# Where tiles lie in SBUF: matmul operands at the bottom, and one 8 KB room for three stages, in a one-core fp32 decoder trunk

## The chip, the cores and the metric

The kernel runs on one core of a Trainium2 chip. The metric is the device time of one execution in microseconds, of which three were taken: 1074.09, 1074.84 and 1077.22, so the median is 1074.84 us. A profile of one execution stands beside them. Its span, from the first to the last instruction, is 1070.4 us.

## The reference

Two layers work on 256 tokens of 1024 channels. Each layer is a half SwiGLU, a mixer and another half SwiGLU, all with a residual. The first mixer is a diagonal state-space model (S5), the second is sparse attention (NSA) over keys and values made after the first layer.

```python
def _swiglu(x, w_in, w_out):
    a, b = jnp.split(x @ w_in, 2, axis=-1)
    return (jax.nn.silu(a) * b) @ w_out
...
    for layer in range(DEPTH):                      # DEPTH = 2, d_model 1024, d_ff 2816
        h = h + 0.5 * _swiglu(_rmsnorm(h, ffn1_norm[layer]), ffn1_w_in[layer], ffn1_w_out[layer])
        u = _rmsnorm(h, mix_norm[layer])
        if layer < N_A_LAYERS:
            h = h + _s5_mixer(u, ...)
        else:
            h = h + _nsa_mixer(u, kv, w_qg[b], q_norm[b], w_o[b], rel_bias)
        h = h + 0.5 * _swiglu(_rmsnorm(h, ffn2_norm[layer]), ffn2_w_in[layer], ffn2_w_out[layer])
        if layer == N_A_LAYERS - 1:
            kv = _shared_kv(h, ...)
```

All of it is fp32.

## The kernel before

**The product of three.** fp32 accuracy comes from splitting each operand into a high and a low part and summing three products (`mm3`, L112 to L117): high activations by high weights (L115), high by low (L116), low by high (L117). The activations are the stationary operand, 128 channels by 128 tokens, loaded by a weight load (PEld) before each matmul. The weights are the moving operand, 512 columns for a full matmul.

**The weights.** Each 1 MB granule comes by one DMA (L70) into one of two buffers `raw`. ScalarE rounds it into `whi` (L86 without a gain, L96 with one) and VectorE subtracts the rest into `wlo` (L92, L99). `whi` and `wlo` have five buffers of 4 KB per partition each, and each buffer holds two slabs of 512 columns.

**The SwiGLU stage** (`ffn`, L177) runs four times: ffn1 of layer 0, ffn2 of layer 0, ffn1 of layer 1, ffn2 of layer 1. Each goes over 11 chunks of 256 hidden channels. A chunk makes 48 matmuls `mm<-whi,xT` and `mm<-wlo,xT` into two accumulators (L222 to L227), from `xT`, the transposed activations (16 KB per partition, high and low). After the fifth slab (k = 4) it also turns the gate product `g` of the chunk before: four transposes on PE (L190), a rounding copy on ScalarE (L140) and a subtraction on VectorE (L141) into `gT` (4 KB, two buffers in the pool `ffn`). At the end of the chunk come the 24 matmuls of the chunk before with `gT` as the stationary operand, `o<-whi,gT` and `o<-wlo,gT`, into four accumulators (`second`, L200). The order on each engine is the order of issue. In the first three passes `background` puts steps of other work into the gaps between slabs: the preparation of S5, the bias tables, what follows the shared projections.

**S5** (`s5`, L487) copies its turned input into `uT` (8 KB, pool `s5r`), drives the states from it (L529, `uT` moving), and closes with a gated product whose stationary operand `yh` lies in the same tile as `xT` (matmuls `ga`, four accumulators). **Attention** (`attention`, L798) turns the probabilities of one head group (L913), copies them into `pt0` (ScalarE, L918) and `pt1` (VectorE, L916), two buffers of 2 KB each, and multiplies them, as the moving operand, by the values (L922). Its output projection has the stationary operand `oT` (matmuls `mm<-..,oT` and `x<-..,oT`, four accumulators). The shared projections (L700, L701) use `xT` again; a third of them goes into the accumulators `kv`.

**Where tiles lie.** Pools are stacked in the order in which they are opened, tiles within a pool in the order of their first use, and a pool that is closed leaves its room to the next one. Counted in KB per partition from the lowest tile of the kernel, the sizes in the code give this layout:

| tile | before |
|---|---|
| `h` (residual), `ident`, `gains` | 0 to 8.7 |
| `xT`, and `yh` of S5 | 8.7 to 24.7 |
| `raw`, two buffers | 24.7 to 40.7 |
| `whi`, five buffers | 40.7 to 60.7 |
| `wlo`, five buffers | 60.7 to 80.7 |
| small tiles | 80.7 to 82.0 |
| `oT` of attention | 138.6 to 154.6 |
| `gT`, last pass | 126.5 to 134.5 |
| `gT`, second and third pass | 169.3 to 177.3 |
| `gT`, first pass | 198.5 to 206.5 |
| `uT` of S5 | 186.2 to 194.2 |
| `pt0`, `pt1` of attention | 198.4 to 206.4 |

Of the kernel before, what the change touches and what calls it, by code (L numbers as in the profile page):

```python
# [9 lines left out]
F32 = mybir.dt.float32  # L10
# [6 lines left out]
P = 128  # L17
# [15 lines left out]
def kernel(ctx: ExitStack, tc: tile.TileContext, A, out):  # L33
    nc = tc.nc
    V, S, G, T = nc.vector, nc.scalar, nc.gpsimd, nc.tensor

    pers = ctx.enter_context(tc.tile_pool(name="pers", bufs=1))
    rawp = ctx.enter_context(tc.tile_pool(name="rawp", bufs=2))
    hip = ctx.enter_context(tc.tile_pool(name="hip", bufs=5))
    lop = ctx.enter_context(tc.tile_pool(name="lop", bufs=5))  # L40
# [12 lines left out]
    # ---- constants and gains  # L53
# [10 lines left out]
    # ---- weights: each granule is split exactly into hi + lo parts as it arrives, scaled by the gain of its rows  # L64
# [13 lines left out]
    def split_half(raw, j, w, gain, k0, eng="av"):  # L78
        """eng: which engines round and subtract"""
# [39 lines left out]
    def gemm(acc, xT, gen, kts=KT, lead=False):  # L119
        """acc[t] = x[t] @ W over kts slabs; lead: token tile 0 goes first in groups of four slabs"""  # L120
# [8 lines left out]
    # ---- 1/rms of the rows of one token tile of h, from its two halves  # L129
# [14 lines left out]
    # ---- h^T as hi and lo parts, channels on partitions, with 1/rms of its rows  # L144
    class Acts:
        def __init__(self, hc):
            self.h = hc
            self.xT = pers.tile([P, 2, KT, 256], F32R, name="xT")
            self.rs = small.tile([P, 2], F32, name="rs", bufs=4)
            self.ss = small.tile([P, 4], F32, name="ss")  # L150
# [15 lines left out]
    def background(bg, n):  # L166
        """n steps of other work, queued behind what has been issued so far"""
# [8 lines left out]
    # ---- res += 1/2 SwiGLU(rmsnorm(h)); done(t, half) once a half of token tile t of res is complete  # L176
    def ffn(x, gi, w_in, w_out, res, perm=False, bg=None, steps=1, done=None, first=()):  # L177
        with tc.tile_pool(name="ffn", bufs=2) as fp, tc.tile_pool(name="ps_a", bufs=1, space=PSUM) as pa:
            xT, rs = x.xT, x.rs
            acc2 = [[pa.tile([P, 512], F32, name=f"o{t}{hf}") for hf in range(2)] for t in range(2)]  # L180
# [3 lines left out]
            def transposed(g):  # L184
                """g^T of one chunk, hi and lo, tokens in natural order"""
                gT = fp.tile([P, 2, 2, 256], F32R, name="gT")
# [31 lines left out]
            for c in range(NCH):  # L218
# [4 lines left out]
                else:  # L223
                    for k in range(KT):
# [3 lines left out]
                        if k == 4:  # L228
                            gT = transposed(prev)
# [12 lines left out]
            second(NCH - 1, transposed(prev))  # L242

    # ---- S5 in chunks of four tokens: discretisation, rotation tables, and stationary operands
# [6 lines left out]
    def s5_prepare(kp, sp, W):  # L251
# [36 lines left out]
        def exp_parts(x):  # L288
            """2^n and exp(r) - 1 with x = n ln2 + r."""
# [53 lines left out]
        def products(x, y, t4_):  # L343
            """x_re y_re, x_im y_im, x_re y_im, x_im y_re"""
# [120 lines left out]
    # ---- h += S5(rmsnorm(h)); token 4 c + 2 t + e is in row 64 e + c of token tile t  # L465
# [651 lines left out]
```

## Time and profile before

| | |
|---|---|
| runs | 1074.09, 1074.84, 1077.22 us |
| span of the profiled execution | 1070.4 us |
| median of the runs less this span | 4.4 us |
| VectorE busy | 708.6 us (66%) |
| ScalarE busy | 574.7 us (54%) |
| GpSimd busy | 180.5 us (17%) |
| HBM read | 165.54 MB, 160 GB/s over the span with what is written |

The profiled execution has no time of its own beside the span; what lies around the span is taken to be the 4.4 us by which the median of the runs exceeds it. The duration of a matmul in the profile is longer than its place in the stream: successive matmuls overlap, so their pace is read from the distance of their starts, and the durations serve to tell groups apart.

### The profile page before, as it was taken

What the parts mean: (1) busy time and instruction counts of PE and PEld (TensorE: products, weight loads), DVE (VectorE), ACT (ScalarE), POOL (GpSimd) and SP (SyncE); (2) the same over time, 40 slices, a digit from 0 to 9 for tenths busy, and PEclk for the clock granted to TensorE, in tenths of its full rate; (3) what the DMA queues carried; (4) which work ended last, traced back from release to release, by engine and by line L of the source; (5) the groups of instructions that cost most, each with busy time, mean ns of one, the idle gap of its engine ahead of it and who ended that gap; (6) DMA issues with size and microseconds to landing.
All of it is one profiled execution on the core that took longest, in us unless ns stands there. A gap on an engine that the chain in (4) does not pass through costs nothing.

```text
span 1070.4 us, 14818 instructions
## 1 busy us (share of the span) xinstructions
PE 1002.3 (94%) x5553; PEld 807.9 (75%) x5553; DVE 708.6 (66%) x1403; ACT 574.7 (54%) x1051; POOL 180.5 (17%) x185
## 2 busy tenths in 40 slices
PE   7978999988879899999999999999977899999998
PEld 6766877876657688887887888887866678888886
DVE  5999755949875465656757555655688866656553
ACT  6443566643335464655665555554786656545451
POOL 6375100305732000000005100000203220000000
PEclk9988999999989999999999999999988999999999
DMA  6553544420328865555464455554303146555551
GB/s 237 183 187 118 197 158 140 163 91 24 137 103 205 331 201 193 197 176 181 170 221 158 158 187 173 191 197 145 100 1 118 40 138 214 170 186 197 185 176 72
DMA packets 27912, 171.74 MB, mean 160 GB/s; under 512 B 4544, under 2 KB 4992, under 8 KB 9024
## 3 DMA queue, kind: packets, MB, share of 16 engines
q1 hardware_dynamic: 26192, 164.77, 44.5%
q0 software_dynamic: 1648, 6.03, 2.2%
q8 instruction: 43, 0.70, 0.3%
q14 instruction: 29, 0.24, 0.1%
HBM read 165.54 MB, written 5.24 MB: 160 GB/s over the span
## 4 chain that ended last, share of the span: by engine, by line
PE 73%; DVE 14%; DMA 4%; ACT 4%; POOL 3%; issue 2%; SPq 0%; ACTq 0%; POOLq 0%; DVEq 0%
PE mm L115 14%; PE mm L116 13%; PE mm L117 13%; PE o L117 7%; PE o L115 7%; PE o L116 7%; DMA raw<-in_w_in_dram 4%; DVE wlo L99 4%; DVE wlo L92 2%; PE tr L190 1%; DVE w L544 1%; ACT whi L96 1%; DVE Pt L906 1%; ACT Pt L895 1%; PE tr L913 1%
## 5 line engine op out<-in xcount | busy, mean ns | idle before, releaser
L99 DVE SCALAR_TENSOR_TENSOR wlo<-raw,gains,whi 128x512 fp32r<-128x512 f32 (+2 forms) x408 | 295.7, 759 | 130.6 <-ACT whi L96 126.7
L96 ACT ACTIVATE whi<-raw,gains 128x512 fp32r<-128x512 f32 (+2 forms) x408 | 267.3, 699 | 187.2 <-PE mm L117 60.8
L115 PE MATMUL mm<-whi,xT 128*128 128x512 f32 (+2 forms) x800 | 313.5, 392 | 4.5 <-ACT whi L96 3.5
L117 PE MATMUL mm<-whi,xT 128*128 128x512 f32 (+2 forms) x800 | 307.1, 384 | 0.0
L116 PE MATMUL mm<-wlo,xT 128*128 128x512 f32 (+2 forms) x800 | 306.8, 384 | 0.3 <-DVE wlo L99 0.3
L92 DVE TENSOR_TENSOR wlo<-raw,whi 128x512 fp32r<-128x512 f32 x192 | 135.0, 743 | 95.3 <-ACT whi L86 95.1
L86 ACT ACTIVATE whi<-raw 128x1024 fp32r<-128x1024 f32 x104 | 108.8, 1057 | 133.6 <-PE mm L117 62.1
L115 PEld LDWEIGHTS mm<-whi,xT 128*128 128x128 f32 x800 | 151.1, 189 | 36.0 <-ACT whi L96 4.8
L117 PEld LDWEIGHTS mm<-whi,xT 128*128 128x128 f32 x800 | 150.9, 189 | 29.8
L116 PEld LDWEIGHTS mm<-wlo,xT 128*128 128x128 f32 x800 | 151.2, 189 | 28.4 <-DVE wlo L99 1.1
L115 PE MATMUL o<-whi,gT 128*128 128x512 f32 x352 | 143.0, 406 | 9.5 <-ACT gT L140 9.5
L117 PE MATMUL o<-whi,gT 128*128 128x512 f32 x352 | 141.6, 404 | 8.1 <-DVE gT L141 7.9
L116 PE MATMUL o<-wlo,gT 128*128 128x512 f32 x352 | 141.4, 402 | 0.0
L115 PEld LDWEIGHTS o<-whi,gT 128*128 128x128 f32 x352 | 67.7, 192 | 27.5 <-ACT gT L140 11.9
L117 PEld LDWEIGHTS o<-whi,gT 128*128 128x128 f32 x352 | 67.6, 192 | 26.3 <-DVE gT L141 10.1
L116 PEld LDWEIGHTS o<-wlo,gT 128*128 128x128 f32 x352 | 67.7, 192 | 15.7
L235 ACT ACTIVATE g<-mm,rs 128x256 f32<-128x256 f32 x88 | 40.7, 471 | 27.7 <-PE mm L117 27.6
L236 DVE SCALAR_TENSOR_TENSOR g<-mm,rs,g 128x256 f32<-128x256 f32 x88 | 41.9, 483 | 19.9 <-ACT g L235 19.4
L141 DVE TENSOR_TENSOR gT<-tr,gT 128x512 fp32r<-128x512 f32 (+1 forms) x55 | 36.4, 661 | 25.9 <-ACT gT L140 25.6
L140 ACT ACTIVATE gT<-tr 128x512 fp32r<-128x512 f32 (+1 forms) x55 | 33.3, 605 | 33.4 <-PE tr L190 26.7
L137 POOL TENSOR_TENSOR rs<-ms,nhalf 128x1 f32<-128x1 f32 x12 | 7.2, 600 | 231.7 <-DVE ms L136 231.6
L895 ACT ACTIVATE Pt<-Pt,mx 128x128 f32<-128x128 f32 (+1 forms) x64 | 28.4, 445 | 6.4 <-DVE mx L890 6.3
(311 smaller groups left out, 1009.1 us busy)
## 6 DMA issues: line engine op xcount, KB each, us to landing
raw<-in_w_in_dram SPq DMA_DIRECT2D x87, 1024.0 KB, 4.9
raw<-in_w_out_dram SPq DMA_DIRECT2D x44, 1024.0 KB, 4.9
raw<-in_w_kv_dram SPq DMA_DIRECT2D x6, 1024.0 KB, 4.8
raw<-in_w_glu_dram SPq DMA_DIRECT2D x4, 1024.0 KB, 4.8
raw<-in_w_o_dram SPq DMA_DIRECT2D x4, 1024.0 KB, 4.9
revd<-rev POOLq DMA_DIRECT2D x8, 384.0 KB, 15.0
raw<-in_w_qg_dram SPq DMA_DIRECT2D x6, 512.0 KB, 3.6
B<-revd POOLq DMA_DIRECT2D x1, 2048.0 KB, 13.2
```

Source lines behind the costliest of these rows:

```text
L86: Last.act = S.activation(hi, r, AF.Copy)
L92: i = el.tensor_tensor(out=lo[:, c], in0=r[:, c], in1=hi[:, c].bitcast(F32), op=ALU.subtract)
L96: Last.act = S.activation(hi[:, c], r[:, c], AF.Identity, scale=g_)
L99: i = V.scalar_tensor_tensor(out=lo[:, c], in0=r[:, c], scalar=g_, in1=hi[:, c].bitcast(F32), op0=ALU.mult, op1=ALU.subtract)
L115: T.matmul(ps, lhsT=xh, rhs=wh, start=start, stop=False)
L116: T.matmul(ps, lhsT=xh, rhs=wl, start=False, stop=False)
L117: Last.pe = T.matmul(ps, lhsT=xl, rhs=wh, start=False, stop=stop_)
L140: i = S.activation(dst_hi, src, AF.Copy)
L141: V.tensor_tensor(out=dst_lo, in0=src, in1=dst_hi.bitcast(F32), op=ALU.subtract)
L235: Last.act = S.activation(sl, acc[t][:, 0:256], AF.Silu, scale=rs[:, t:t + 1])
L236: Last.dve = V.scalar_tensor_tensor(out=g[:, t, :], in0=acc[t][:, 256:512], scalar=rs[:, t:t + 1], in1=sl, op0=ALU.mult, op1=ALU.mult)
L895: S.activation(Pt[:, r, br], Pt[:, r, br], AF.Exp, scale=-1.0, bias=mx[:, c:c + 1], accum_out=sm[:, c:c + 1])
```

## The change

Nothing that is computed changes, and no instruction is added or taken out by intent. Three things are done to the tiles.

1. A new pool `low` is opened first. It takes `xT` (and `yh`) out of `pers`, and a new tile `turned` of 8 KB. After it come `whi` (`hip`) and `wlo` (`lop`), then `pers` with `h`, `ident` and `gains`, then `raw`.
2. `turned` is one room for three stages. Each pass of `ffn` takes it for `gT`, the chunk's parity choosing the half; S5 takes it for `uT`; attention takes it for its four turned blocks, used in rotation.
3. The pool `s5r` and the tiles `gT`, `pt0`, `pt1` of the old pools go.

```diff
+    low = ctx.enter_context(tc.tile_pool(name="low", bufs=1))
+    hip = ctx.enter_context(tc.tile_pool(name="hip", bufs=5))
+    lop = ctx.enter_context(tc.tile_pool(name="lop", bufs=5))
     pers = ctx.enter_context(tc.tile_pool(name="pers", bufs=1))
     rawp = ctx.enter_context(tc.tile_pool(name="rawp", bufs=2))
-    hip = ctx.enter_context(tc.tile_pool(name="hip", bufs=5))
-    lop = ctx.enter_context(tc.tile_pool(name="lop", bufs=5))
...
+    def turn_room():
+        return low.tile([P, 2, 1024], F32R, name="turned")
...
-            self.xT = pers.tile([P, 2, KT, 256], F32R, name="xT")
+            self.xT = low.tile([P, 2, KT, 256], F32R, name="xT")
...
+            gTs = turn_room()
...
-            def transposed(g):
-                gT = fp.tile([P, 2, 2, 256], F32R, name="gT")
+            def transposed(c, g):
+                gT = gTs[:, c % 2].rearrange("p (i f c) -> p i f c", i=2, f=2)
...
-                            gT = transposed(prev)
+                            gT = transposed(c - 1, prev)
...
-            second(NCH - 1, transposed(prev))
+            second(NCH - 1, transposed(NCH - 1, prev))
...
-        with tc.tile_pool(name="s5r", bufs=1) as rp, tc.tile_pool(name="s5w", bufs=2) as wp, \
+        with tc.tile_pool(name="s5w", bufs=2) as wp, \
...
-            uT = rp.tile([P, NG, NC], F32, name="uT")
+            uT = turn_room().bitcast(F32).rearrange("p b (g c) -> p (b g) c", c=NC)
...
-            yh = pers.tile([P, 2, KT, 256], F32R, name="xT")
+            yh = low.tile([P, 2, KT, 256], F32R, name="xT")
...
+            pt_room, turn = turn_room().bitcast(F32).rearrange("p b (k c) -> p (b k) c", c=512), [0]
...
-                        pts.append(tp.tile([P, 512], F32, name=f"pt{br}"))
+                        pts.append(pt_room[:, turn[0] % 4])
+                        turn[0] += 1
```

By the sizes in the code the layout becomes, in the same count: `xT` 0 to 16, `turned` 16 to 24, `whi` 24 to 44, `wlo` 44 to 64, `h` 64 to 72, `ident` and `gains` to 72.7, `raw` 72.7 to 88.7. Everything above is 8 KB higher than before, less what `gT`, `uT`, `pt0` and `pt1` took there. `oT`, `g`, and the operands of S5 other than `uT` stay high. The other lines of the diff take out comments.

## The prediction

> **What bounds the kernel now.** I read the page's head and slices first, then the chain of waits, then stretches of one pass, then single matmuls in order of time.
>
> ```profile
> span 1070.4 us, 14818 instructions
> PE 1002.3 (94%) x5553; PEld 807.9 (75%) x5553; DVE 708.6 (66%) x1403; ACT 574.7 (54%) x1051; POOL 180.5 (17%) x185
> PE   7978999988879899999999999999977899999998
> by line: PE mm L115 13.7%; PE mm L116 13.5%; PE mm L117 13.4%; PE o L117 7.0%; PE o L115 7.0%; PE o L116 6.9%; DMA raw<-in_w_in_dram 4.0%; DVE wlo L99 3.6%; issue 1.9%; DVE wlo L92 1.6%; PE tr L190 1.4%; DVE w L544 1.3%; ACT whi L96 1.1%; D
> ```
>
> TensorE is busy 94% of the span, and the six groups of SwiGLU matmuls make 61.5% of the chain that ended last. Outside the first four slices, S5 (slices 9 to 12) and attention (30 to 32) the row of TensorE stands at 8 or 9. Two stretches from inside the passes show what the other engines have left:
>
> ```profile
> 390.00:500.00 110.00, 110.00 (x495) 90.20 (x495) 66.88 (x104) 60.43 (x90) 0.00 (x0) 1.00 0.55 190
> 901.00:918.00 17.00, 17.00 (x78) 13.91 (x77) 9.91 (x16) 8.90 (x14) 0.00 (x0) 1.00 0.55 186
> ACT whi L86 <- PE mm L117: 62.1, 38, 6.8
> ACT whi L96 <- PE mm L117: 60.8, 49, 2.5
> ACT whi L86 <- PE o L117: 36.5, 25, 1.5
> ACT whi L96 <- PE o L117: 24.7, 17, 5.4
> ```
>
> In a chunk of 17 us TensorE has no gap, while VectorE works 9.91 us, ScalarE 8.90 and the DMA engines 55%. ScalarE waits 62.1 + 60.8 + 36.5 + 24.7 = 184.1 us for TensorE to give weight buffers back: the weights are ahead. So a pass costs what its matmuls cost, and the question is whether their price hangs on where their operands lie.
>
> **The one thing the change can reach.** All full matmuls have one shape, 128 by 128 stationary and 512 columns moving, yet they fall into two classes:
>
> ```profile
> L115 PE MATMUL kv<-whi,xT x16: 389/389/389, 527.5 to 537.7; 128*128 128x512 f32 x16
> L115 PE MATMUL mm<-whi,xT x800: 276/389/797, 7.9 to 1052.9; 128*128 128x512 f32 x147, 128*128 128x256 f32 x9, 128*128 128x304 f32 x4
> L115 PE MATMUL o<-whi,gT x352: 388/396/792, 34.5 to 1065.4; 128*128 128x512 f32 x176
> L115 PE MATMUL x<-whi,oT x16: 390/392/398, 851.5 to 876.6; 128*128 128x512 f32 x16
> 531.79 0.39 PE L116 MATMUL kv<-wlo,xT 128*128 128x512 f32 x1
> ...
> 538.14 0.39 PE L117 MATMUL kv<-whi,xT 128*128 128x512 f32 x1
> 622.07 0.39 PE L115 MATMUL o<-whi,gT 128*128 128x512 f32 x1
> ...
> 627.68 0.39 PE L115 MATMUL mm<-whi,xT 128*128 128x512 f32 x1
> ...
> 629.07 0.39 PE L115 MATMUL mm<-whi,xT 128*128 128x512 f32 x1
> 851.51 0.39 PE L115 MATMUL x<-whi,oT 128*128 128x512 f32 x1
> ...
> 854.31 0.39 PE L115 MATMUL x<-whi,oT 128*128 128x512 f32 x1
> 271.96 0.39 PE L117 MATMUL ga<-whi,xT 128*128 128x512 f32 x1
> ...
> 273.10 0.39 PE L116 MATMUL ga<-wlo,xT 128*128 128x512 f32 x1
> ```
>
> (min/median/max in ns; then starts in us.) With `xT` as the stationary operand the median is 389 ns, with `gT` 396, with `oT` 392. The pace shows the same. From 531.79 to 538.14 lie 28 steps of the `kv` run: 6.35 / 28 = 226.8 ns. From 622.07 to 627.68 lie the 24 of one `o` run: 5.61 / 24 = 233.8 ns. From 851.51 to 854.31 lie 12 of `oT`: 2.80 / 12 = 233.3 ns. After an `o` run the first six `xT` matmuls still take 1.39 us (627.68 to 629.07) instead of 6 x 226.8 = 1.36.
>
> What tells the classes apart? Not the moving weights: all read the same buffers `whi` and `wlo`. Not the number of accumulators: `ga` alternates over four, as `o` and `oT` do, and runs 271.96 to 273.10 in 5 steps at 228 ns, the fast class. Not the shape of the stationary tile: `oT` is laid out as `xT` is. Left is the place: `xT` lies at 8.7 to 24.7 KB, `gT` at 126 KB and above, `oT` at 138.6 KB. The trace cannot say whether height, or distance from the weights at 40.7 to 80.7 KB, makes the difference. The change ends both: `gT` comes to 16 to 24 KB, wholly inside the room that `xT` has today, just below the weights.
>
> [...]
>
> **The sum, part by part.**
>
> *`gT` low.* 24 x (233.8 - 226.8) = 0.168 us per run of 24. The recovery behind it gives up to 0.03 us more; I take 0.02, since a run still begins after a wait in places. Together 0.188 us a chunk. How many of the 44 runs count? The `o` lines hold 7.0 + 7.0 + 6.9 = 20.9% of the chain, 223.7 us; by 0.2338 that is 957 matmuls, 39.9 runs. Some of these ran at a lowered clock in the first pass (0.93 between 50 and 100 us, row below), which inflates the figure, so 38: 38 x 0.188 = 7.1 us. Nothing is late in its place: the next chunk's weights have the 184.1 us of waiting in hand, and per 17 us only 0.19 of it is used.
>
> *`xT`, `whi`, `wlo` low.* All move down by 8.7 to 16.7 KB. The 16 `kv` rows of L115 go over eight slabs, which is four of the five `whi` buffers, and all of them take 389, so the place of the moving weights has shown no price and I take 0. Bounds: the recoveries vanish altogether, as much again as the 0.02 a chunk, about -1 us; or the pace slips to the other class, which is the slower rival.
>
> *`uT`, `pt` low; `ident`, `h`, `gains`, `raw` high.* These change the moving operand of small matmuls and the sources of ScalarE and VectorE:
>
> ```profile
> L529 PE MATMUL dr<-uT,WBT 128*128 128x64 f32 x128 | 16.4, 277 | 2.3 <-ACT uT L518 1.4 <-issue 0.7 <-DVE uT L516 0.2
> L922 PE MATMUL x<-pt,Vt 128*64 128x256 f32 x72 | 11.8, 412 | 0.8 <-DVE pt L916 0.8
> L190 PE MATMUL tr<-ident,g 128*128 128x128 f32 x176 | 26.8, 275 | 0.0
> L140 ACT ACTIVATE gT<-tr 128x512 fp32r<-128x512 f32 x33 | 19.6, 593 | 21.5 <-PE tr L190 21.4
> L140 ACT ACTIVATE xT<-tr 128x512 fp32r<-128x512 f32 x16 | 9.3, 590 | 14.8 <-PE tr L156 14.7
> L141 DVE TENSOR_TENSOR gT<-tr,gT 128x512 fp32r<-128x512 f32 x33 | 22.7, 689 | 17.1 <-ACT gT L140 17.0
> L141 DVE TENSOR_TENSOR xT<-tr,xT 128x512 fp32r<-128x512 f32 x16 | 10.9, 689 | 9.2 <-ACT xT L140 9.2
> L918 ACT ACTIVATE pt<-tr 128x512 f32<-128x512 f32 x12 | 7.1, 595 | 3.2 <-PE tr L913 3.1
> 50.00:100.00 50.00, 39.72 (x162) 31.07 (x160) 47.44 (x53) 19.98 (x32) 36.60 (x31) 0.93 0.47 158
> ```
>
> For TensorE I bound by the ratio of the two classes, 7.0 / 226.8 = 3.1%: `uT` and `pt` gain at most 3.1% of 16.4 + 11.8 = 0.9 us, the transposes with `ident` higher lose at most 3.1% of 26.8 = 0.8 us. For the other engines the same copy costs 593 ns to a high `gT` and 590 to a low `xT`, the same subtraction 689 and 689: no price of place. I take 0 for all of this, being nearest to those rows; where VectorE leads (47.44 of 50 us in the last row), 0.5% would be 0.5 us over the first 100 us either way.
>
> *One room instead of buffers.* Does it add a wait? Half c of `turned` is written behind transposes of chunk c - 1, which stand on TensorE behind the 24 matmuls that read the other half; TensorE works in order, so even if the whole room were guarded as one, the copy waits for nothing new. `uT` is written behind transposes that follow the last `o` matmul. In attention the four blocks rotate as two times two buffers did. If the copies of a pair (L918, L916) were put one behind the other there, VectorE's would start up to 0.595 us later, 12 times, 7.1 us; queued behind it are VectorE's scalings for the next group, and L922 waits for it. The blocks are disjoint, as are the halves of a `whi` buffer, so 0 is my value.
>
> Sum: -7.1 us. The profiled span would go from 1070.4 to 1063.3; with the 4.4 us around it, which nothing here touches, 1067.7 against the median of 1074.8.
>
> **The rivals.**
>
> *No change: the slow class belongs to the `o` work itself* and not to its place, say to operands written shortly before. For it: `gT` and `oT` are both made from products a moment earlier. Against it: `yh` of the fast `ga` run is made in the same way. Time 1074.8, or within 3 us of it. [...] A shared room that orders the attention copies (7.1 us back) gives nearly the same time.
>
> *Only part arrives: the supply becomes the bound.* Where the weights lead by little (second and third pass with background work) half of the gain would end as a wait of TensorE for L96 or L99: 1074.8 - 3.5 = 1071.3. Against it: 8.90 of 17 us.
>
> *Slower: the fast class is a matter of the pair.* If the pace hangs on how stationary and moving addresses stand to each other, the new pair could be a bad one for `xT`. Place: the `mm` runs. Price: their 13.7 + 13.5 + 13.4 = 40.6% of the chain is 434.6 us, 434.6 / 0.2268 = 1916 matmuls, x 7.0 ns = 13.4 us; with the `o` runs still gaining, 1074.8 + 13.4 - 7.1 = 1081; without, 1088. It decides from the first chunk on, as soon as the median of `mm` leaves 389. Against it: the four `whi` buffers of the `kv` run stand at four distances from `xT` without a trace of it.
>
> **How the numbers follow.** The forecast has 0.76, its own range 1065.5 to 1070 (7.1 us plus or minus the bounds of 0.5 to 1 us each and the spread of the runs). Partial arrival has 0.05, no change 0.11, slower 0.08. The range that holds 8 in 10 reaches from 1064, where the recoveries and `uT` and `pt` all gain too, to 1074.5, which takes in partial arrival and part of the no-change case. What can be told from no change is about 0.3%, 3.2 us, that is below 1071.6: faster 0.80 with more than half of the partial case, same 0.12, slower 0.08.
>
> **What would show it.** Right: `o` matmuls (named `o<-whi,turned` then) at a median of 389 instead of 396 and a pace near 227 ns; `mm` unchanged at 389; 0.19 us less per chunk; `x<-whi,oT` still at 392 and 233 ns, since `oT` stays high. A fast `oT` would say that place is not the cause; slow `o` at 16 to 24 KB would end my theory; TensorE gaps before L115 inside the passes would be the supply; `mm` off 389 the bad pair.

## The result and the profile after

| | median | runs |
|---|---|---|
| before, run again beside it | 1075.54 us (1072.27 to 1079.12) | 22 |
| after | 1072.88 us (1069.73 to 1078.71) | 22 |
| ratio | 0.9976, 95% interval 0.9966 to 0.9986 | |

The change saves 2.7 us of a forecast 7.1: not slower, but no more than the 0.3% that counts as no change here. The head of the profile after, first the page's own lines (span and busy time of each engine):

```profile
span 1071.0 us, 14818 instructions
PE 1004.4 (94%) x5553; PEld 814.9 (76%) x5553; DVE 705.8 (66%) x1403; ACT 575.6 (54%) x1051; POOL 181.9 (17%) x185
```

The profiled execution itself took 1072.76 us, so 1.8 us lie around its span, and not 4.4. The span of before (1070.4) belonged to a quick execution: its runs' median less 1.8 would be a span of about 1073.7.

Next, single lines of the code in the profile after (minimum, median and maximum of the duration in ns, then the first and last start), as they stand in the prediction for before:

```profile
L121 PE MATMUL kv<-whi,xT x16: 389/389/389, 529.7 to 539.9; 128*128 128x512 f32 x16
L121 PE MATMUL mm<-whi,xT x800: 278/389/795, 10.4 to 1053.7; 128*128 128x512 f32 x147, 128*128 128x256 f32 x9, 128*128 128x304 f32 x4
L121 PE MATMUL o<-whi,turned x352: 387/389/628, 37.0 to 1066.0; 128*128 128x512 f32 x176
L121 PE MATMUL x<-whi,oT x16: 392/394/400, 854.1 to 879.2; 128*128 128x512 f32 x16
```

And one run of 24 in order of time, its first matmul and the first of the next chunk:

```profile
624.03 0.39 PE L121 MATMUL o<-whi,turned 128*128 128x512 f32 x1
...
629.24 0.39 PE L123 MATMUL o<-whi,turned 128*128 128x512 f32 x1
629.47 0.39 PE L121 MATMUL mm<-whi,xT 128*128 128x512 f32 x1
```

The `o` matmuls have gone from a median of 396 to 389 ns, and their pace from 233.8 to 5.44 / 24 = 226.7 ns. `mm` and `kv` stayed at 389; `oT`, which stayed high, stayed slow (394). This is what the prediction asked for, line by line. Yet the sum did not arrive. To see where it went, the span is cut at the first and the last `o` matmul of each pass (their starts in the trace), which gives the four passes, the attention between the third and the fourth, and the rest (start, S5, shared projections, tail). The kernels of the later sections stand in the same table, so that they can be compared; each row is one profiled execution. The column "equal" says whether, in the passes, the stationary tile and `whi` start at the same address modulo 256 bytes; the experiments show why that is asked. The column behind it names the engine that makes the `wlo` part of `w_o`, the weights of attention's output projection: these 16 subtractions (L92) are the only ones of the kernel's weights that GpSimd makes, while the description of the kernel gives them all to VectorE.

| kernel | order of pools | equal | w_o's subtraction | four passes | attention | rest | span |
|---|---|---|---|---|---|---|---|
| before | old | no | GpSimd | 716.0 | 145.8 | 208.6 | 1070.4 |
| before_again | old | no | GpSimd | 719.9 | 146.6 | 210.0 | 1076.5 |
| after | new | yes | GpSimd | 709.2 | 148.1 | 213.7 | 1071.0 |
| after_again | new | yes | GpSimd | 710.7 | 149.5 | 212.9 | 1073.1 |
| order_only | new | first pass | GpSimd | 718.2 | 150.1 | 212.5 | 1080.8 |
| room_only | old, room lowest | no | GpSimd | 716.3 | 147.1 | 209.3 | 1072.7 |
| aligned_high | old | yes | GpSimd | 710.4 | 148.4 | 209.4 | 1068.2 |
| residues | old | first pass | GpSimd | 714.2 | 145.7 | 214.1 | 1074.0 |
| after_off | new | no | GpSimd | 717.2 | 149.9 | 210.4 | 1077.5 |
| raw_first | new, raw lowest | yes | GpSimd | 712.8 | 150.1 | 209.8 | 1072.7 |
| aligned_nudge | old | yes | GpSimd | 709.1 | 148.1 | 209.6 | 1066.8 |
| after_nudge | new | yes | GpSimd | 709.8 | 149.9 | 209.6 | 1069.3 |
| before_av | old | no | VectorE | 714.0 | 141.4 | 212.0 | 1067.4 |
| before_av2 | old | no | VectorE | 714.2 | 141.6 | 214.1 | 1069.9 |
| aligned_av | old | yes | VectorE | 712.3 | 142.0 | 210.5 | 1064.8 |
| off_av | new | no | VectorE | 714.5 | 141.6 | 210.3 | 1066.4 |
| after_av | new | yes | VectorE | 709.5 | 142.1 | 212.5 | 1064.1 |
| after_av2 | new | yes | VectorE | 709.4 | 142.0 | 210.6 | 1062.0 |

Read the first four rows. The passes lost 5.3 to 10.7 us, depending on which two are compared. Most of that spread is the second pass of `before_again`, which ran at a granted clock of 0.97 where that of `before` and `after` had 0.99. The attention grew by 1.5 to 3.7 us and the rest by 2.9 to 5.1. So the question has two parts: was it really the height that made the passes quicker, and what outside the passes took some of it back?

### The profile page after: what moved, and what is told of

Its sections match the earlier page's. It is cut to its first block, busy times and chain, and to the rows that moved or that the text cites. A ratio compares the mean times of both kernels' runs of the same rounds, so it can differ in the third digit from the quotient of the medians.

```text
span 1071.0 us, 14818 instructions
## 1 busy us (share of the span) xinstructions
PE 1004.4 (94%) x5553; PEld 814.9 (76%) x5553; DVE 705.8 (66%) x1403; ACT 575.6 (54%) x1051; POOL 181.9 (17%) x185
## 4 chain that ended last, share of the span: by engine, by line
PE 70%; DVE 15%; DMA 5%; ACT 4%; POOL 3%; issue 2%; SPq 0%; ACTq 0%; POOLq 0%; DVEq 0%
PE mm L121 13%; PE mm L122 13%; PE mm L123 13%; PE o L123 6%; PE o L121 6%; PE o L122 6%; DVE wlo L105 3%; DMA raw<-in_w_in_dram 3%; DVE wlo L98 2%; DMA raw<-in_w_out_dram 2%; PE tr L197 1%; DVE Pt L914 1%; ACT whi L102 1%; DVE w L551 1%; POOL hy L267 1%
## 5 line engine op out<-in xcount | busy, mean ns | idle before, releaser
L92 ACT ACTIVATE whi<-raw 128x1024 fp32r<-128x1024 f32 x104 | 108.9, 1060 | 130.2 <-PE mm L123 52.2
L121 PE MATMUL o<-whi,turned 128*128 128x512 f32 x352 | 140.6, 399 | 8.3 <-ACT turned L146 8.2
L123 PE MATMUL o<-whi,turned 128*128 128x512 f32 x352 | 140.0, 399 | 8.7 <-DVE turned L147 8.5
L122 PE MATMUL o<-wlo,turned 128*128 128x512 f32 x352 | 138.9, 395 | 0.0
L123 PEld LDWEIGHTS o<-whi,turned 128*128 128x128 f32 x352 | 67.4, 191 | 25.7 <-DVE turned L147 11.8
L121 PEld LDWEIGHTS o<-whi,turned 128*128 128x128 f32 x352 | 67.5, 192 | 25.1 <-ACT turned L146 11.3
L122 PEld LDWEIGHTS o<-wlo,turned 128*128 128x128 f32 x352 | 67.4, 191 | 13.8
L242 ACT ACTIVATE g<-mm,rs 128x256 f32<-128x256 f32 x88 | 40.7, 471 | 26.8 <-PE mm L123 26.7
L147 DVE TENSOR_TENSOR turned<-tr,turned 128x512 fp32r<-128x512 f32 (+1 forms) x55 | 36.4, 661 | 23.1 <-ACT turned L146 22.8
L146 ACT ACTIVATE turned<-tr 128x512 fp32r<-128x512 f32 (+1 forms) x55 | 33.4, 607 | 31.6 <-PE tr L197 24.7
```

The lines of the kernel that those rows point to most:

```text
L92: Last.act = S.activation(hi, r, AF.Copy)
L121: T.matmul(ps, lhsT=xh, rhs=wh, start=start, stop=False)
L122: T.matmul(ps, lhsT=xh, rhs=wl, start=False, stop=False)
L123: Last.pe = T.matmul(ps, lhsT=xl, rhs=wh, start=False, stop=stop_)
L146: i = S.activation(dst_hi, src, AF.Copy)
L147: V.tensor_tensor(out=dst_lo, in0=src, in1=dst_hi.bitcast(F32), op=ALU.subtract)
```

## The experiments

### First set: the two halves of the change, and both kernels again

All runs beside five rounds of the kernel before; its median in this set is 1076.73 us. `before_again` and `after_again` are the two kernels unchanged.

> The kernel before, unchanged, for a second profile and for what two equal kernels differ by. Ratio 1.000 within 0.2%. If the profile of before was a quick execution, this span lies above 1070.4, nearer 1073.7 (the median of its 22 runs, 1075.5, less the 1.8 us that lie around the span in the runs of the changed kernel). Stages to compare: to the first gT matmul 34.5 us in the old profile and 37.0 in the changed kernel; S5 with the start of the second pass 110.0 and 112.5; attention with the start of the last pass 145.8 and 148.1. If these three differences are chance, the values here scatter between the two; if they belong to the new layout, they repeat 34.5, 110.0 and 145.8.

Measured: 1.0006 (0.9992 to 1.0019), 1077.24 us.

> The changed kernel, unchanged. Ratio 0.9976 again, within 0.1 to 0.2%. The pace of the full matmuls with the low stationary operand repeats (median 389 ns, 24 in 5.44 us, a chunk in 16.79 us): sure by every theory. If the loss outside the passes belongs to the layout, the three stages repeat 37.0, 112.5 and 148.1 us; if it is chance they scatter.

Measured: 0.9965 (0.9951 to 0.9980), 1072.51 us. The gain is there again, 1072.51 us against 1076.73 beside it: 4.2 us, where 2.7 were found first.

`order_only` opens the pools in the new order, with `xT` in `low`, but leaves `gT`, `uT` and `pt` in their old, high pools:

```diff
+    low = ctx.enter_context(tc.tile_pool(name="low", bufs=1))
+    hip = ctx.enter_context(tc.tile_pool(name="hip", bufs=5))
+    lop = ctx.enter_context(tc.tile_pool(name="lop", bufs=5))
     pers = ctx.enter_context(tc.tile_pool(name="pers", bufs=1))
     rawp = ctx.enter_context(tc.tile_pool(name="rawp", bufs=2))
-    hip = ctx.enter_context(tc.tile_pool(name="hip", bufs=5))
-    lop = ctx.enter_context(tc.tile_pool(name="lop", bufs=5))
...
-            self.xT = pers.tile([P, 2, KT, 256], F32R, name="xT")
+            self.xT = low.tile([P, 2, KT, 256], F32R, name="xT")
```

> Only the order of the pools: xT, split weights lowest, residual and raw weights above; gT, uT and the turned blocks of attention in their old pools, high. Theory A (moving residual, identity and raw weights up costs about 4 us outside the passes): ratio 1.003 to 1.005, gT matmuls at 396 ns and 17.0 us a chunk. Theory B (the shared room costs it) and theory C (the quicker passes shift what comes after): ratio 1.000, the same 396 ns.

`room_only` keeps the old order and puts the shared room, alone in `low`, below everything:

```diff
+    low = ctx.enter_context(tc.tile_pool(name="low", bufs=1))
     pers = ctx.enter_context(tc.tile_pool(name="pers", bufs=1))
     rawp = ctx.enter_context(tc.tile_pool(name="rawp", bufs=2))
...
-                gT = fp.tile([P, 2, 2, 256], F32R, name="gT")
+                gT = gTs[:, c % 2].rearrange("p (i f c) -> p i f c", i=2, f=2)
```

> Only the room of 8 KB, lowest of all, shared by gT, uT and the turned blocks; residual, xT, raw and split weights follow in the old order. gT matmuls at 389 ns, 16.79 us a chunk by all theories. Theory A: the whole gain arrives, ratio 0.993 to 0.994. Theory B and theory C: 0.9975, as in the changed kernel; B shows waits at the first copies into the room in S5 or attention, C shows longer stages without such waits.

Measured: `order_only` 1.0018 (1.0003 to 1.0034), 1078.26 us; `room_only` 0.9981 (0.9965 to 0.9998), 1074.64 us. The totals fit none of the three theories. `order_only` lies between the 1.003 to 1.005 of theory A and the 1.000 of B and C, and `room_only` lies at the 0.9975 of B and C, where A asks for 0.993 to 0.994. The matmuls did not look like any theory either. In `order_only`, the lines of `o` pass by pass (first, second, third, fourth):

```profile
L121 PE MATMUL o<-whi,gT x88: 387/389/628, 35.3 to 230.5; 128*128 128x512 f32 x88
L121 PE MATMUL o<-whi,gT x88: 393/398/792, 344.0 to 521.6; 128*128 128x512 f32 x88
L121 PE MATMUL o<-whi,gT x88: 393/396/496, 581.7 to 760.9; 128*128 128x512 f32 x88
L121 PE MATMUL o<-whi,gT x88: 392/395/502, 911.4 to 1075.9; 128*128 128x512 f32 x88
```

and in `room_only`, with the room at the very bottom:

```profile
L121 PE MATMUL o<-whi,turned x352: 389/395/792, 34.2 to 1067.8; 128*128 128x512 f32 x176
```

In `order_only` `gT` is fast in the first pass (389 ns), where it lies highest of all (198 KB), and slow in the others (395 to 398). In `room_only` it is at 0 KB and slow (395). Height is not the cause. "Slow `o` at 16 to 24 KB would end my theory", the prediction says; slow `o` at 0 to 8 KB does.

What does fit is found by laying the tiles out from the sizes in the code and taking, for each pair, the start of the stationary tile less the start of `whi`, in bytes modulo 512 (the slices within the tiles step by multiples of 512, so one number holds for a tile):

| pair | modulo 512 | class |
|---|---|---|
| `xT` before, after, `order_only`, `room_only` | 0 | fast |
| `turned` after | 0 | fast |
| `gT` of `order_only`, first pass | 0 | fast |
| `gT` of `order_only`, second and third, fourth | 320, 32 | slow |
| `gT` before, first, second and third, fourth | 288, 96, 320 | slow |
| `turned` of `room_only` | 288 | slow |
| `oT` before, after | 384, 96 | slow |

Neither start decides by itself: `turned` starts at a multiple of 512 bytes in `after`, where it is fast, and in `room_only`, where it is slow, and `whi` is shared by fast and slow products in every kernel. So the rival theory for the next set: a matmul is fast when its stationary and its moving operand start at one place modulo 512 bytes.

### Second set: the pair against the height, and the place of raw

The median of before is 1075.24 us here. `aligned_high` is the kernel before with pads, that is unused bytes ahead of a tile, and nothing else; every buffer stays in its old pool. The pads of the four passes have 224, 416, 416 and 192 bytes, that ahead of `oT` 128:

```diff
-    def ffn(x, gi, w_in, w_out, res, perm=False, bg=None, steps=1, done=None, first=()):
+    def ffn(x, gi, w_in, w_out, res, perm=False, bg=None, steps=1, done=None, first=(), pad=0):
         with tc.tile_pool(name="ffn", bufs=2) as fp, tc.tile_pool(name="ps_a", bufs=1, space=PSUM) as pa:
+            if pad:
+                fp.tile([P, pad // 4], F32, name="pad", bufs=1)
...
+            ap.tile([P, 32], F32, name="pad")
             oT = ap.tile([P, 2, KT, 256], F32R, name="oT")
```

> The old kernel with every buffer in its old pool and at its old height; only pads of 128 to 416 bytes are put ahead of `gT` and `oT`, so that each starts at the weights' place modulo 512 bytes. Theory of the pair (the pace hangs on whether the stationary and the moving operand start at one place modulo 512 bytes): `o<-whi,gT` at 226.7 to 227.5 ns a matmul and 399 ns long (before: 233.5, 406) although `gT` lies at 143 to 214 KB, `x<-whi,oT` at 227 and 389 (before 233, 392), passes 7 us shorter, nothing outside them: 0.9925 to 0.994 of the time before (about 7 to 8 us less). Theory of the height (that of the prediction): 233.5 ns as before and a ratio of 0.999 to 1.001.

`residues` has the same pads in `ffn` with other sizes (480, 32, 480, 128 bytes) and none ahead of `oT`.

> As the kernel before, with other pads: `gT` starts 256 bytes past the weights' place modulo 512 in the first pass, 128 in the second, 64 in the third and 448 in the fourth; `oT` stays 384 past it. Theory of the pair with a step of 512: all four passes at 233 to 234 ns, ratio 0.999 to 1.001. With a step of 256: the first pass alone at 227, ratio 0.998 to 0.999. With a pace that falls off with the distance: between 227 and 233.5, another value in each pass. Theory of the height: as before in all.

`after_off` is the changed kernel with the shared room begun 288 bytes later:

```diff
-        return low.tile([P, 2, 1024], F32R, name="turned")
+        room = low.tile([P, 2176], F32R, name="turned")
+        return room[:, 72:2120].rearrange("p (b c) -> p b c", b=2)
```

> The changed kernel with the shared room as low as it was, but begun 288 bytes past the weights' place modulo 512, as `gT` was in the old first pass; all else in the change's order. Theory of the pair: `o` back at 233 to 234 ns, the passes' gain of 7 us gone and the cost outside them left, so 1.003 to 1.006 of the time before. Theory of the height: `o` at 227, 0.995 to 0.998 as the changed kernel.

Measured: `aligned_high` 0.9969 (0.9951 to 0.9988), 1072.28 us; `residues` 0.9985 (0.9967 to 1.0002), 1073.41 us; `after_off` 1.0031 (1.0011 to 1.0051), 1079.18 us. The lines of `aligned_high`, with `gT` at 126 KB and above and `oT` at 138 KB:

```profile
L115 PE MATMUL o<-whi,gT x352: 387/389/628, 34.6 to 1063.3; 128*128 128x512 f32 x176
L115 PE MATMUL x<-whi,oT x16: 389/389/397, 851.4 to 876.4; 128*128 128x512 f32 x16
```

of `after_off`, low but shifted:

```profile
L122 PE MATMUL o<-whi,turned x352: 392/395/796, 36.8 to 1072.6; 128*128 128x512 f32 x176
```

and of `residues`, pass by pass (256, 128, 64 and 448 bytes off), the last row being L117 of the fourth pass, low activations by high weights:

```profile
L115 PE MATMUL o<-whi,gT x88: 387/389/632, 35.1 to 231.0; 128*128 128x512 f32 x88
L115 PE MATMUL o<-whi,gT x85: 390/395/792, 346.3 to 516.8; 128*128 128x512 f32 x85
L115 PE MATMUL o<-whi,gT x86: 391/394/501, 580.0 to 757.8; 128*128 128x512 f32 x86
L115 PE MATMUL o<-whi,gT x88: 392/392/505, 905.4 to 1069.0; 128*128 128x512 f32 x88
L117 PE MATMUL o<-whi,gT x88: 388/388/400, 905.9 to 1069.5; 128*128 128x512 f32 x88
```

The theory of the height is gone from both sides: 128 to 416 bytes of padding make high operands fast (389 ns), 288 bytes make low ones slow (395). The step in these runs is 256, not 512: the first pass of `residues` is fast at 256 off (389), while 64 and 128 are slow (394 and 395), and 448 (192 modulo 256) lies in between, with L117 as fast as any and L115 3 ns behind. That 256 is enough rests on one pass: its durations, and its runs of 24, whose starts lie 234.3 ns apart there as in the first pass of `aligned_high` (234.3) and not as in that of `before` (237.8). Between `after_off` and `after_again`, each against the before of its own set, lie 1.0031 - 0.9965 = 0.0066, 7.1 us, with some 2.7 us either way by the two intervals. That it is the forecast to the digit is chance.

But `aligned_high` falls short: its passes take 710.4 us against 716.0 to 719.9, and the total gains only 3.0 us. It has the old order of the pools, so the new order can't be what takes the rest.

`raw_first` asks whether the place of `raw` matters. It is the changed kernel with this pool opened first:

```diff
+    rawp = ctx.enter_context(tc.tile_pool(name="rawp", bufs=2))
     low = ctx.enter_context(tc.tile_pool(name="low", bufs=1))
...
     pers = ctx.enter_context(tc.tile_pool(name="pers", bufs=1))
-    rawp = ctx.enter_context(tc.tile_pool(name="rawp", bufs=2))
```

> The changed kernel with the raw weights' pool put below everything, so that `raw` is about as low as, or lower than, it was; the transposed operands, the room and the split weights follow in the change's order and keep one place modulo 512 bytes, the residual and the identity stay above. If the place of `raw` is what costs time outside the passes (late first weights, the attention's late scaling of `Pt`): passes as in the changed kernel (7 us less than before), the rest as before, ratio 0.993 to 0.995. If it is the residual's and identity's place: 0.9965 as the changed kernel. If the outside cost belongs to no buffer but to the run of things in time: between, without a pattern that follows `raw`.

Measured: 0.9990 (0.9974 to 1.0005), 1073.11 us, 2.1 us below the median of before. It gives no sign that a low `raw` helps: attention 150.1 us, as with a high one.

### What the table says about the attention

With GpSimd in the attention's projection, the table has two clusters: 145.7 to 147.1 us (`before` twice, `room_only`, `residues`) and 148.1 to 150.1 us (all others). The line that goes with them is VectorE's scaling of `Pt`. Here is the point where the profiles part, in order of time (start, duration), in `before_again`:

```profile
834.86 0.28 DVE L906 TENSOR_SCALAR Pt<-Pt,sm 128x128 f32<-128x128 f32 x1
834.89 1.37 POOL L92 TENSOR_TENSOR wlo<-raw,whi 128x512 fp32r<-128x512 f32 x1 [0.23 <-ACT whi L86]
835.06 0.68 DVE L916 COPY pt<-tr 128x512 f32<-128x512 f32 x1
835.79 0.65 PE L922 MATMUL x<-pt,Vt 128*64 128x256 f32 x4 [0.79 <-DVE pt L916]
```

and in `after_again`:

```profile
830.18 1.36 DVE L914 TENSOR_SCALAR Pt<-Pt,sm 128x128 f32<-128x128 f32 x1
830.19 1.27 POOL L98 TENSOR_TENSOR wlo<-raw,whi 128x512 fp32r<-128x512 f32 x1 [0.21 <-ACT whi L92]
831.47 0.68 DVE L925 COPY turned<-tr 128x512 f32<-128x512 f32 x1
```

Before, VectorE's scaling starts 30 ns ahead of GpSimd's subtraction, takes its 0.28 us, and GpSimd's takes 1.37 us instead of 1.27. After, it starts 10 ns ahead and takes 1.36 us: it ends when GpSimd's subtraction has ended (831.54 us against 831.46). The copy behind it starts 0.17 us after GpSimd's subtraction in the one and 1.28 us after it in the other, and TensorE waits for that copy (0.79 us in the one, 1.90 in the other). All scalings of `before` and `after` that take over 1.1 us look like this one: each starts between 27 ns before and 197 ns after the start of a subtraction on GpSimd and ends 81 to 155 ns after its end. What makes the one wait for the other is not shown. At this place the scaling starts 23 to 32 ns ahead in the four profiles of the lower cluster and 1 to 17 ns in the eight of the upper one. That is no general threshold: some 20 us earlier, at a scaling of 128x256, a lead of 27 ns loses in `before` (1.44 us) and one of 80 ns wins in `after_again` (0.36 us).

The groups of the two kernels (busy time, mean ns, then TensorE's or VectorE's idle time before them) show the same. `before_again`:

```profile
L906 DVE TENSOR_SCALAR Pt<-Pt,sm 128x128 f32<-128x128 f32 (+1 forms) x64 | 24.0, 422 | 0.2
L922 PE MATMUL x<-pt,Vt 128*64 128x256 f32 x72 | 12.0, 419 | 0.8 <-DVE pt L916 0.8
```

`after_again`:

```profile
L914 DVE TENSOR_SCALAR Pt<-Pt,sm 128x128 f32<-128x128 f32 (+1 forms) x64 | 25.1, 439 | 0.2
L931 PE MATMUL x<-turned,Vt 128*64 128x256 f32 x72 | 11.9, 416 | 1.9 <-DVE turned L925 1.9
```

The mean of the scalings is 422 ns in all four profiles of the lower cluster and 438 or 439 in all eight of the upper one. The profiles of the one lie 1.0 to 4.4 us above those of the other, of which the wait accounts for 1.1 us. What is beyond that goes with a lower clock right behind the wait. The whole attention of `before_again` as one stretch (length, busy time of PE, PEld, DVE, ACT and POOL, granted clock of TensorE, share of the DMA engines, GB/s):

```profile
760.10:906.70 146.60, 129.76 (x766) 102.08 (x765) 111.14 (x378) 102.26 (x274) 30.59 (x30) 0.95 0.29 98
```

and of `after_again`:

```profile
755.90:905.40 149.50, 132.08 (x767) 103.80 (x765) 112.35 (x379) 102.43 (x274) 29.50 (x26) 0.93 0.28 96
```

TensorE does the same matmuls in 2.3 us more, at a granted clock of 0.93 instead of 0.95. The mean over the stage does not decide: `room_only` has 0.93 as well and takes 147.1 us. What differs is where the clock falls. In all eight profiles of the upper cluster the granted clock goes to one half for 6.8 us from 76 to 78 us after the attention's start, about 2 us behind the start of the late copy; in none of the lower one does it do so there. The stretch from 77.6 to 84.4 us in `before_again`, and then in `after_again`:

```profile
837.70:844.50 6.80, 5.38 (x28) 4.64 (x28) 6.49 (x32) 4.76 (x19) 2.26 (x2) 1.00 0.46 154
833.50:840.30 6.80, 5.87 (x22) 4.79 (x21) 5.74 (x22) 4.63 (x16) 1.66 (x2) 0.50 0.45 154
```

When the matmuls of the two attentions are laid side by side, those of `after_again` are 0.5 us early at 74 us, 0.7 late at 79 (the wait), 2.7 late at 83 (the half clock) and 2.9 at the end. So the whole difference arises within 10 us around this meeting.

### Third set: moving the race, and taking it away

The median of before is 1076.53 us. Two kernels, `aligned_nudge` and `after_nudge`, try to tip this race of two engines for the first start with one small GpSimd memset of a pad:

```diff
             for j in range(2):
+                if nudge is not None and (n, j) == (1, 1):
+                    G.memset(nudge, 0.0)
                 hi, lo = split_half(raw, j, w, gain, ((n % 2) * 2 + j) * 2, eng)
```

Two, `before_av` and `after_av`, take it away by giving w_o's subtractions to VectorE:

```diff
-            gen = granules([A["w_o"][j] for j in range(KT // 2)], eng='ag')
+            gen = granules([A["w_o"][j] for j in range(KT // 2)], eng='av')
```

> As the run with the old order and the operands of the passes and of the projection at one place modulo 512 bytes, with one GpSimd memset of 128x32 more, put between the two halves of w_o's second granule, so that GpSimd asks for its third subtraction later than VectorE for its last scaling of `Pt`. Theory of the race (a start 30 ns later of that scaling is what gives back part of the passes' gain): the scalings' mean falls from 439 to 422 ns, the copy of `pt` on VectorE is no longer 1.1 us late, the attention takes 145.5 to 147 us in place of 148.4, and the ratio is 0.993 to 0.9955. If the race is only a sign of something else in the attention: 148 to 150 us there, and 0.9965 to 0.9975.

> The changed kernel with the same memset (and a pad of 512 bytes to hold it). Theory of the race: scalings at 422 ns, attention 145.5 to 147 us in place of 148.1 to 149.5, ratio 0.9935 to 0.996, still some 1 us behind the old order for the later start. If the order costs elsewhere: 0.9965 as the changed kernel, attention 148 to 150.

Measured: `aligned_nudge` 0.9960 (0.9941 to 0.9978), 1071.40 us; `after_nudge` 0.9973 (0.9957 to 0.9989), 1073.85 us. Both miss their aim. The scalings stay at a mean of 438 ns and the attention at 148.1 and 149.9 us. The reason is in the place of the memset, in `aligned_nudge` and in `after_nudge`:

```profile
L109 POOL MEMSET pad<- x1: 116/116/116, 752.5 to 752.5; 128x32 f32 x1
L115 POOL MEMSET pad<- x1: 120/120/120, 745.4 to 745.4; 128x32 f32 x1
```

The subtractions that it was to put off start at 824.18 and 826.41 us. The memset ran 72 and 81 us earlier, long before GpSimd's first subtraction for w_o, so these two runs do not test the race. What they give is a second execution of the two kernels they are made from.

> The kernel before with w_o's 16 subtractions on VectorE in place of GpSimd, so that the two no longer meet there: the base for the next run. 16 x 743 ns more on VectorE and no scaling of `Pt` held up: between 0.998 and 1.004 by either theory.

> The changed kernel with the same edit as the run before this. Theory of the race: with no race to lose, the attention takes the same in both within 0.7 us, and this run stands 5 to 7 us below the run before it (0.994 to 0.9955 of it). If the cost belongs to the order: the attention is 2 to 4 us longer here, and this run stands 3 to 4 us below.

Measured: `before_av` 0.9936 (0.9913 to 0.9959), 1069.95 us; `after_av` 0.9895 (0.9872 to 0.9918), 1065.91 us. The first is outside what was expected of it (0.998 to 1.004): the old kernel gains 6.6 us too. Its traces say why. In `before` seven of the 64 scalings take over 1.1 us, in `after` eight, and in `before_av` none: the engines meet in more places than the one above, and the change had added one. With it gone, the attentions of the two are 141.4 and 142.1 us, where they had been 1.5 to 3.7 us apart. The difference of the totals, 4.0 us (as a ratio of the single runs 0.9958, interval 0.9941 to 0.9975), is still short of 5 to 7, so the square of both questions was run in one set.

### Fourth set: order by pair, with no race

The median of before is 1075.95 us. `before_av2` and `after_av2` are the two kernels above once more; `aligned_av` and `off_av` are `aligned_high` and `after_off` with the same edit of the projection.

> The kernel before with w_o's subtractions on VectorE, once more, as the corner of the square (old order, operands apart): 1069 to 1071 us, 0.9925 to 0.995 of the time before, attention 141 to 142.5 us.

> Old order, operands of the passes and the projection at one place modulo 512, w_o's subtractions on VectorE. Race theory: nothing is given back now, so the whole of the pair's price stands: 5.5 to 7.5 us below the run before this, attention 141 to 142 us. Order theory says the same of this run, since the order is the old one. If quicker passes give time back wherever they end (something later in phase): 3 to 4 us below.

> New order, the shared room 288 bytes off, w_o's subtractions on VectorE. Race theory: the order alone costs at most 1 us (the later start): 0 to 1 us above the first run of this call, attention 141 to 142.5 us. Order theory: 3 to 4 us above it, as the same kernel stood with GpSimd in the attention.

> The changed kernel with w_o's subtractions on VectorE, once more. Race theory: 5 to 7 us below the first run of this call, 0 to 1.5 above the second. Order theory: 3 to 4 us below the first, 3 to 4 above the second.

| median us (ratio to before, interval) | apart | equal |
|---|---|---|
| old order | `before_av2` 1071.11 (0.9955, 0.9938 to 0.9972) | `aligned_av` 1065.58 (0.9898, 0.9878 to 0.9918) |
| new order | `off_av` 1070.35 (0.9950, 0.9932 to 0.9968) | `after_av2` 1063.88 (0.9895, 0.9877 to 0.9912) |

Along a row, the pair is worth 5.5 us in the old order (by the single runs 0.9944, interval 0.9922 to 0.9965) and 6.5 in the new (0.9940, 0.9921 to 0.9959). Down a column, the order is worth 0.8 and 1.7 us, both in favour of the new one and both within the scatter: `off_av` stands to `before_av2` as 0.9997, interval 0.9977 to 1.0018, and `after_av2` to `aligned_av` as 0.9994, interval 0.9975 to 1.0013. So the order of the pools costs nothing that these runs can tell, and the 3 to 4 us which it seemed to cost belonged to the attention. The attentions of the four take 141.6, 142.0, 141.6 and 142.0 us. The groups of `after_av2` show that TensorE no longer waits for the copy:

```profile
L914 DVE TENSOR_SCALAR Pt<-Pt,sm 128x128 f32<-128x128 f32 (+1 forms) x64 | 16.7, 312 | 0.1
L931 PE MATMUL x<-turned,Vt 128*64 128x256 f32 x72 | 12.6, 417 | 0.1
L98 DVE TENSOR_TENSOR wlo<-raw,whi 128x512 fp32r<-128x512 f32 x208 | 146.3, 743 | 92.4 <-ACT whi L92 92.3
```

and its attention stretch, in the columns used above:

```profile
752.00:894.00 142.00, 129.60 (x766) 101.43 (x766) 109.79 (x395) 102.15 (x274) 9.23 (x10) 0.96 0.30 101
```

VectorE takes over 16 subtractions, which add 10.3 us to it in this stage, and is still busy for less time than in `before_again` (109.79 us against 111.14): the scalings fall from 24.0 to 16.7 us, and four groups that write `qs`, `qst`, `sm` and `pst` fall by 3.8 us together. At 1063.88 us, `after_av2` beats both kernels; `aligned_av`, which is the old layout with a few hundred bytes of padding, is the same within the scatter.

## Why the prediction went as it did

**What bounds the kernel, and the price of a matmul: right.** The two classes were real, and the price of 7.0 ns was right (233.8 to 226.7). The third pass went from 179.8 to 177.8 us and the fourth from 165.3 to 163.2; 11 runs by 0.188 would be 2.07. Nothing was late in its place: ScalarE still waited for TensorE to give buffers back. These rows of the waits after (total, count, longest) are the four that made 184.1 us before, now 58.9 + 52.2 + 34.4 + 23.5 = 169.0:

```profile
ACT whi L102 <- PE mm L123: 58.9, 48, 2.5
ACT whi L92 <- PE mm L123: 52.2, 35, 1.7
ACT whi L92 <- PE o L123: 34.4, 25, 1.4
ACT whi L102 <- PE o L123: 23.5, 17, 5.3
```

**How many runs count (38 of 44): too many.** Over the profiles of the table, seven with unequal tiles in all four passes and nine with equal ones, the four passes take 716.0 and 710.4 us on average: 5.6 us, not 7.1. By pass these are 0.8, 1.1, 1.8 and 1.9 us. In the first pass the matmuls of a run start 237.8 ns apart with unequal tiles and 234.2 with equal ones (the median run of each profile), which is half of the step of the other passes; there many runs begin behind a wait. The second pass scatters with its granted clock, 0.97 to 0.99, so its 1.1 us is a rough figure.

**The cause: wrong.** The step that failed in the mechanism is "Left is the place". The rival that the prediction called a matter of the pair had the mechanism, although it was priced as a loss. What was held against it, that "the four `whi` buffers of the `kv` run stand at four distances from `xT` without a trace of it", could not decide: these buffers are 4096 bytes apart, so all four distances leave one remainder modulo 256. A test of distance has to vary the remainder too. That the `o` matmuls came out at the forecast pace was luck: the change's sizes happen to put `turned` at the same remainder as `whi` (both follow `xT` by multiples of 512 bytes), while in `room_only`, where the room lies lower still, they stay at 395 ns.

**`xT`, `whi`, `wlo` low at 0: right,** for a reason that was not seen: the three move together and keep their remainder.

**"The slow class belongs to the `o` work itself": wrong.** In `aligned_high` pads alone take `gT` from a median of 396 to 389 ns and `oT` from 392 to 389.

**"I take 0 for all of this" (`ident`, `h`, `gains`, `raw`, `uT`, `pt`): right for the price of each operation, and the step that lost most of the gain.** The transposes with `ident` hold 26.8 us after as before:

```profile
L197 PE MATMUL tr<-ident,g 128*128 128x128 f32 x176 | 26.8, 275 | 0.0
```

What the step left out is that the attention's timing needn't stay as it was. There GpSimd and VectorE meet within tens of nanoseconds, and in the changed kernel the meeting falls the other way: 1.1 us of waiting, and 1.5 to 3.7 us in the stage. So the passes gave about 5.6 of the forecast 7.1 us, and the attention took back about half of that (on average 149.3 us in the upper cluster against 146.3 in the lower), at a place that no edit of the change was meant to touch. Taken away in both kernels, the meeting leaves a difference of 4.0 us in one set and 7.2 in the other. The rest outside the passes was 2.9 to 5.1 us longer in the profiles after; over all 18 it lies between 208.6 and 214.1 and goes neither with the order nor with the pair (`before_av2`, old order, 214.1; `off_av`, new order, 210.3), and is 210.7 us on average with unequal tiles and 211.0 with equal ones, so this is taken for scatter between executions.

**One room instead of buffers at 0: right.** `room_only` has the room and nothing else, and stands at 0.9981 (0.9965 to 0.9998).

**"4.4 us around it": wrong, without effect on the sum.** 1.7 to 1.8 us lie around the span in every run that has both. The difference was that of a quick execution from the median.

Three things stay open. What shifts the meeting by some 20 ns from one layout to another is not known; `aligned_high` differs from before by pads alone and falls on the slower side, `residues` with other pads doesn't. That the half clock in the attention follows from the longer wait was only seen together with it, not tried by itself; the memset that was to turn the meeting alone ran too early to do so. That this one meeting takes the gain back is therefore shown by its place in the traces and by the runs that remove all meetings at once, not by a run that turns it alone. And why the distance modulo 256 counts, and how much each one costs between 32 and 224, is open beyond the rows above.

## What to carry to other kernels

When operands of one shape run in two speed classes, compare their start addresses modulo small powers of two before their heights, and try a pad of some hundred bytes before a new layout: here 128 to 416 bytes in front of `gT` and `oT` gained as much as the whole reordering (0.9969 against 0.9976 and 0.9965). When a change with a sure local gain brings half of it, cut the span into stages and look for instructions of one group that take several times as long as the others and end just after one of another engine (here 1.36 us in place of 0.28). Here that place was worth more than the change: w_o's subtractions on VectorE gave 0.9936 and 0.9955 by themselves.

## What the runs showed of the hardware

In this case the pace of a full matmul (128 by 128 stationary, 512 columns of fp32r moving) went with how the two operands' start addresses in the partition stand to each other. In full runs behind the first pass it was 226.7 ns where they are equal modulo 512 bytes (`after`, `aligned_high`), and 232.9 to 233.9 at distances of 32, 64 and 96 bytes modulo 256 (`after_off`, `before`). In durations, equal tiles had a median of 389 ns; a distance of 128 had 395, and 192 had 392 for one product of the three and 388 for another (`residues`). A distance of 256 was run in the first pass alone and was fast there (389 ns, `residues`). Height in the partition did not decide: 389 ns at 198 KB (first pass of `order_only`), 395 at 0 KB (`room_only`). And where VectorE and GpSimd met, a scaling that started 30 ns ahead of GpSimd's subtraction took 0.28 us (`before_again`), and one that started 10 ns ahead took 1.36 (`after_again`), with a wait of TensorE of 1.90 us in place of 0.79; in all eight profiles of the second kind 6.8 us of half clock on TensorE followed.
